# Score blocks of two directions in one TensorE run, and small products on VectorE instead of GpSimd, in a bidirectional recurrent mixer

## The chip, the cores and the metric

The kernel runs on one core of a Trainium2 chip. A core has a matrix engine (TensorE, PE in the profile, its weight loads PEld), VectorE (DVE), ScalarE (ACT), GpSimd (POOL), and queues that issue transfers between the main memory and the on-chip memories (SBUF, and PSUM for matrix products). The metric is the device time of one execution in microseconds (us).

## The reference

Two layers of a trunk: layer 0 mixes tokens by windowed attention, layer 1 by a bidirectional gated linear recurrence (HGRN2). Each mixer also carries four cross-attention heads into 256 memory tokens, and each layer ends with a convolutional feed-forward part. The change is in layer 1's mixer alone. There are 1024 tokens and 8 heads, with 128 keys and 128 values a head.

```python
def gla_chunked(q, k, v, log_f):          # chunks of 16 tokens
    b = jnp.cumsum(log_f, axis=2)
    q_dec, k_dec, k_end = q * jnp.exp(b), k * jnp.exp(-b), k * jnp.exp(b[:, :, -1:] - b)
    s = jnp.where(causal, jnp.einsum('bcthk,bcshk->bchts', q_dec, k_dec), 0.0)
    o_intra = jnp.einsum('bchts,bcshv->bcthv', s, v)
    # step over the chunks: o_inter = q_dec @ state; state = exp(b_end) * state + k_end^T v
    return o_intra + o_inter

o = gla_chunked(q, k_f, v, lf_f) + flip_t(gla_chunked(flip_t(q), flip_t(k_b), flip_t(v), flip_t(lf_b)))
o = rmsnorm(o, norm_g) * silu(gate)
```

with `f = lb + (1 - lb) * sigmoid(z)`, `log_f = log(f)`, `k = 1 - f` for each of the two directions (z from a projection of its own), and `q` passed through silu.

## The kernel before

**Stages.** The program does the memory's keys and values, layer 0's mixer (`window`), its output projection and feed-forward part, then layer 1's mixer (`hgrn`, from about 1205 to 1872 us), its output projection (`wo1.finish`) and the second feed-forward part. The large products split each fp32 operand into a high and a low part and take three products (`mm3`, lines 84 to 86). Their weights are split on arrival: ScalarE casts the high part (line 79), VectorE subtracts (line 80).

**A head of the mixer.** `proj(h)` makes queries, the two gates' inputs (`proj_fm`) and, for two heads at a time, values and output gates (`proj_tm`) into PSUM banks `pj`. ScalarE and VectorE take them out (lines 1091 to 1093, 1113, 1115, 1129, 1134). `head(h)` then goes through four directions: (forward, first half of the tokens), (backward, second half), (forward, second half), (backward, first half); `d` is 0 for forward and 1 for backward, `b` the half. After that it makes the outputs of the two halves (`output`). In every second head, cross-attention units run behind the third and the fourth direction (`cross`).

**A direction** works on 512 tokens, as four quarters `c` of 128, tokens along the free axis and the 128 keys on the partitions. ScalarE and VectorE make the decays inside chunks of 16: `EP` from the chunk's start, `ER` to its end (lines 1177 to 1192). The scores inside a quarter are built from blocks of decay levels. `E1`, `E2` (lines 1204 to 1209) hold decayed queries and keys for the 32 x 32 diagonal blocks. `step(n)` (lines 1219, 1220) doubles the length over which `ER` and `EP` reach. After it, a tile `G` holds in its later halves the decayed queries (line 1227, on GpSimd) and in its earlier halves the decayed keys (line 1228, on VectorE): `G32` for blocks between neighbours of 32 tokens, `G` for blocks between neighbours of 64.

`block(c, i, j, x, y, n)` (line 1212) is one product of 128 rows by 32 stationary columns. It writes PSUM partitions i to i+31 and n columns from j of quarter c, in the direction's bank `PA[d]`, and sits at array columns i to i+31: the array's columns are used as four groups of 32, at i = 0, 32, 64 and 96. Per quarter there are two blocks of 64 columns (from `G`), four diagonal ones of 32, and two of 32 (from `G32`). `lt` and `er` are 1 and 0 for a forward direction and 0 and 1 for a backward one. So the blocks of `G` lie in the groups at 0 and 32 for forward and at 64 and 96 for backward; those of `G32` lie at 0 and 64 for forward and at 32 and 96 for backward.

After the blocks VectorE copies the causal part of the bank to `Az[d]` (`copy_predicated`, line 1253). `As[b]`, the sum of both directions' scores, takes it: a ScalarE copy for the first direction of a half (line 1257), a GpSimd addition for the second (line 1259). GpSimd also makes the decayed query `qin` (line 1251). A transpose of the decayed key, products with the values and the state updates `S` follow (lines 1262 to 1276). `output` multiplies `As`, `qin` and `S` (line 1291) and normalizes.

**Buffers.** `E()` gives one of five tiles of the tag "E" in turn: a direction takes eight (`a_`, `L1`, `R`, `B`, `E1`, `E2`, `G32`, `G`), and one is reused when its last reader is done. `PA` is one bank for each direction, `As` has two tiles.

**What sets the order.** The code is written once, head after head. A planner with a timeline of its own (`schedule_with_timeline_sim=True`) then gives each engine a fixed order from its own estimates of durations; engines wait on semaphores. `tc.high_priority(AHEAD)` lets instructions go ahead of others that are ready, and `tc.issue_after(x)` keeps instructions behind `x` in the order.

Of the kernel before, what the change touches and what calls it, by code (L numbers as in the profile page):

```python
# [8 lines left out]
F32 = mybir.dt.float32  # L9
F32R = mybir.dt.float32r  # L10
# [3 lines left out]
ALU = mybir.AluOpType  # L14
# [4 lines left out]
P = 128  # L19
# [30 lines left out]
def build(tc, A, out):  # L50
    nc = tc.nc
    act, dve, pool, pe = nc.scalar, nc.vector, nc.gpsimd, nc.tensor
# [970 lines left out]
    def hgrn():  # L1023
# [3 lines left out]
        early = tc.alloc_tile_pool(name="hg0", bufs=1, reuse_waits="tile")  # L1027
# [4 lines left out]
        late = tc.alloc_tile_pool(name="hgv", bufs=1, side="right", reuse_waits="tile")  # L1032
        V, G = [late.tile([P, 3, NT, P], F32, name=x) for x in ("v", "gs")]
        wp = tc.alloc_tile_pool(name="hg1", bufs=1, side="right", reuse_waits="tile")
        for x in ("xh", "xl", "ph", "pl"):
            wp.tile([P, 512], F32R, tag=x, bufs=1, name=x)
        for x in ("kvh", "kvl"):
            wp.tile([P, 2, 256], F32R, tag=x, bufs=1, name=x)
# [120 lines left out]
            r["run"] = run  # L1159
            return r  # L1160

        def direction(h, r, d, b, qin, S, As):

            q, k = r["q"][b], r["s"][d][b]
            rev = slice(None, None, -1) if d else slice(None)
# [2 lines left out]
            def E():  # L1168
                return early.tile([P, 512], F32, tag="E", bufs=5, name="E")
# [51 lines left out]

            for n in (32, 64):
                step(n // 2)
                G = E()
                gl, ge = halves(G, n)
                pl_, pe_, rl_, re_, ql, qe, kl, ke = parts(n)
                pool.tensor_tensor(gl, pl_, ql, op=ALU.mult)
                dve.tensor_tensor(ge, re_, ke, op=ALU.mult)
                if n == 32:
                    G32 = G  # L1230
            with tc.high_priority(AHEAD):
                far, near, x = er * 64 + er * 32, er * 64 + lt * 32, lt * 64
                mm = None
                for c in range(4):
                    with tc.issue_after(mm.ins) if mm else nullcontext():
                        block(c, far, x, G, G, 64)
                        block(c, near, x, G, G, 64)
                        for o in (0, 32):
                            block(c, x + o, x + o, E2, E1)
                        mm = block(c, x + er * 32, x + lt * 32, G32, G32)  # L1240
                for c in range(4):
                    with tc.issue_after(mm.ins):
                        block(c, far, far, E2, E1)
                        block(c, near, near, E2, E1)
                        mm = block(c, far, near, G32, G32)
            step(64)
            dec = wp.tile([P, 4], F32, tag="dec", bufs=2, name="dec")
            e = 0 if d else P - 1
# [1 line left out]
            bs = slice(b * 512, (b + 1) * 512)  # L1250
            sum_steps[1].send(pool.tensor_tensor(qin[:, bs], EP, q, op=ALU.mult))
            dve.tensor_tensor(ER, ER, k, op=ALU.mult)
            dve.copy_predicated(Az[d], gm[d], pa.rearrange("p c t -> p (c t)"))
            a2 = lambda x: x.rearrange("p c t -> p (c t)")
            if As[b] is None:
                As[b] = wp.tile([P, 4, P], F32, tag="As", bufs=2, name="As")
                act.copy(a2(As[b]), Az[d])
            else:
                pool.tensor_tensor(a2(As[b]), a2(As[b]), Az[d], op=ALU.add)
            tp = bank("pt")  # L1260
            for c in range(4):
                pe.transpose(tp[:, c, :], ER[:, c * P:(c + 1) * P], ident)
# [5 lines left out]
            for c in (range(3, -1, -1) if d else range(4)):  # L1268
                cg = 4 * b + c
                nx = cg - 1 if d else cg + 1  # L1270
                if not 0 <= nx < NT:
                    continue
                if cg == (NT - 1 if d else 0):
                    act.copy(S[:, nx, :], pu[:, c, :])
                else:
                    dve.scalar_tensor_tensor(S[:, nx, :], S[:, cg, :], dec[:, c:c + 1], pu[:, c, :],
                                             op0=ALU.mult, op1=ALU.add)

        def output(h, r, b, qin, S, As):
            po = bank("po")  # L1280
# [45 lines left out]

        def cross(n):
            def pair(kind, i):
                return [wp.tile([P, 512], F32R, tag=kind + c, bufs=1, name=kind + c) for c in "hl"]

            for _ in range(n):
                xh_, xb_ = units.pop(0)
                if xhead[1] != xh_:
                    xhead[1] = xh_
                    xhead[0] = cross_head(1, xh_, wp)
                cross_unit(1, xh_, xb_, xhead[0], wp, tags, wp, pair, not units)

        def head(h, r):
            qin = [wo1.wf.tile([P, T], F32, tag=f"qin{d}", bufs=1, name="qin") for d in range(2)]
            S = [wp.tile([P, NT, P], F32, tag=f"S{d}", bufs=1, name="S") for d in range(2)]  # L1340
            As = [None, None]
            for i, (d, b) in enumerate(((0, 0), (1, 1), (0, 1), (1, 0))):
                direction(h, r, d, b, qin[d], S[d], As)
                if i < len(r["later"]):
                    r["run"](r["later"][i])
                cross(HX[h][i])
                if h == 7 and i == 1:
                    wo1.load(0, n=RING)
            if h == 7:
                early.release()  # L1350
                es.release()
                eq.release()
                wo1.open()
            for i, b in enumerate((1, 0)):
                output(h, r, b, qin, S, As)
                cross(HX[h][4 + i])
# [220 lines left out]
```

## Time and profile before

| | |
|---|---|
| median of 3 runs | 2629.17 us (2628.51 to 2630.56) |
| profiled execution, its own time | 2632.24 us |
| its span, first to last instruction | 2630.4 us |
| TensorE busy in the span | 2593.7 us, 99% |
| mixer of layer 1, 1205 to 1872 us: TensorE, VectorE, ScalarE, GpSimd busy | 658.31, 523.60, 354.51, 175.28 us |
| score blocks (line 1212), TensorE busy | 36.4 us, 2048 records |

A row of groups reads: line, engine, operation, output<-inputs, shapes, count | busy time in us, mean of one in ns | idle time of the engine just before, and what ended it. A row of stretches gives the length and then the busy time of each engine with its number of instructions, the granted TensorE clock (1.00 is full), the share of the transfer engines and GB/s. A row in order of time gives start, duration, engine, line, operation and count. A product in fp32 leaves two records, one for each pass.

### The profile page before, as it was taken

To read this page: it belongs to the slowest core of one execution; us is meant where nothing else is said; L and a number is where in the kernel's file an instruction comes from. 1 tells how busy PE (TensorE), PEld (TensorE's weight loads), DVE (VectorE), ACT (ScalarE), POOL (GpSimd) and SP (SyncE) were. 2 spreads that over 40 slices of the span, in tenths; PEclk is the share of its full clock that TensorE was granted. 3 is DMA by queue.
4 is the path that set the end of the run, shared out by engine and by line. 5 is a ranking of instruction groups with operands and counts; after the bars stand their busy time and mean duration, and the time that the engine had idled before them with its cause. 6 is when DMAs were issued, how large, how long until landed. Compare 5 with 4: busy or idle time off the path is not lost. (4 is left out here: it accounts for less than half of the span.)

```text
span 2630.4 us, 39132 instructions
## 1 busy us (share of the span) xinstructions
PE 2593.7 (99%) x14596; PEld 2174.2 (83%) x14596; DVE 1763.4 (67%) x2807; ACT 1333.4 (51%) x2395; POOL 476.4 (18%) x552
## 2 busy tenths in 40 slices
PE   8999999999999999999999999999999999999998
PEld 7988887888888888887888888888887888888887
DVE  6677775577555664488697796877657665656447
ACT  6566665444444454465555554556434444444453
POOL 0431110211111100032233131222311011110013
PEclk9999999999999999999999999999999999999999
DMA  9782341567787757673246341113337777775666
GB/s 356 258 199 67 103 146 57 168 171 195 192 210 201 198 160 250 194 267 109 70 151 162 75 99 47 55 49 101 120 119 197 190 201 200 205 200 172 215 193 236
DMA packets 203919, 431.18 MB, mean 164 GB/s; under 512 B 20048, under 2 KB 64464, under 8 KB 198096
## 3 DMA queue, kind: packets, MB, share of 16 engines
q1 hardware_dynamic: 169744, 329.30, 38.4%
q0 software_dynamic: 24544, 90.19, 16.4%
q10 hardware_dynamic: 9440, 9.19, 1.1%
q8 instruction: 114, 1.87, 0.3%
q14 instruction: 77, 0.63, 0.1%
HBM read 333.18 MB, written 119.54 MB: 172 GB/s over the span
## 5 line engine op out<-in xcount | busy, mean ns | idle before, releaser
L90 DVE TENSOR_TENSOR wl<-st,wh 128x1024 fp32r<-128x1024 f32 (+1 forms) x238 | 263.3, 1113 | 318.8 <-ACT wh L89 294.4
L89 ACT CAST wh<-st 128x1024 fp32r<-128x1024 f32 (+1 forms) x238 | 222.6, 937 | 293.1 <-PE X L578 194.1
L84 PE MATMUL pj<-uh,wh 128*128 128x512 f32 x512 | 202.9, 397 | 3.6 <-DVE q L1129 2.5
L578 PE MATMUL X<-wl,wh 128*128 128x512 f32 x528 | 204.7, 390 | 0.3 <-DVE wl L90 0.3
L578 PE MATMUL X<-wh,wl 128*128 128x512 f32 x528 | 204.5, 389 | 0.0
L86 PE MATMUL pj<-uh,wl 128*128 128x512 f32 x512 | 202.1, 395 | 0.0
L85 PE MATMUL pj<-ul,wh 128*128 128x512 f32 x512 | 201.0, 393 | 0.1
L578 PE MATMUL X<-wh 128*128 128x512 f32 x528 | 198.7, 390 | 1.4 <-ACT c L992 1.4
L84 PE MATMUL pj<-wh,uh 128*128 128x384 f32 (+1 forms) x512 | 189.0, 370 | 2.5 <-DVE gs L1115 1.9
L86 PE MATMUL pj<-wh,ul 128*128 128x384 f32 (+1 forms) x512 | 187.1, 365 | 0.0
L85 PE MATMUL pj<-wl,uh 128*128 128x384 f32 (+1 forms) x512 | 187.0, 365 | 0.0
L80 DVE TENSOR_TENSOR wl<-st,wh 128x1024 fp32r<-128x1024 f32 (+1 forms) x91 | 119.1, 1316 | 29.7 <-ACT wh L79 28.9
L578 PE MATMUL V<-uh,wh 128*128 128x512 f32 x336 | 130.7, 389 | 0.0
L578 PE MATMUL V<-ul,wh 128*128 128x512 f32 x336 | 130.7, 389 | 0.0
L578 PE MATMUL V<-uh,wl 128*128 128x512 f32 x336 | 130.7, 389 | 0.0
L578 PEld LDWEIGHTS X<-wh 128*128 128x128 f32 x528 | 99.1, 188 | 22.4 <-ACT c L992 1.8
L578 PEld LDWEIGHTS X<-wl,wh 128*128 128x128 f32 x528 | 99.1, 188 | 21.1 <-DVE wl L90 0.7
L578 PEld LDWEIGHTS X<-wh,wl 128*128 128x128 f32 x528 | 99.1, 188 | 20.5
L84 PEld LDWEIGHTS pj<-uh,wh 128*128 128x128 f32 x512 | 96.3, 188 | 23.4 <-DVE q L1129 3.3
L79 ACT CAST wh<-st 128x1024 fp32r<-128x1024 f32 (+1 forms) x97 | 97.5, 1014 | 35.3 <-PE pj L85 22.3
L961 POOL TENSOR_TENSOR c<-c,g 128x512 f32<-128x512 f32 x24 | 42.5, 1789 | 391.2 <-PE X L578 322.1
L85 PEld LDWEIGHTS pj<-ul,wh 128*128 128x128 f32 x512 | 96.3, 188 | 19.3 <-DVE ul L90 0.4
(409 smaller groups left out, 7058.8 us busy)
## 6 DMA issues: line engine op xcount, KB each, us to landing
st<-hid SPq DMA_DIRECT2D x154, 256.0 KB, 3.0
st<-in_ffw_dram SPq DMA_DIRECT2D x108, 256.0 KB, 3.2
w2s<-in_ffw_dram POOLq DMA_DIRECT2D x24, 1024.0 KB, 8.3
st<-in_ffw_dram SPq DMA_DIRECT2D x46, 512.0 KB, 4.2
hid<-tt SPq DMA_DIRECT2D x88, 256.0 KB, 4.8
st<-w2s SPq DMA_DIRECT2D x88, 256.0 KB, 2.8
sx<-in_ffw_dram SPq DMA_DIRECT2D x84, 256.0 KB, 3.9
sy<-in_ffw_dram SPq DMA_DIRECT2D x42, 512.0 KB, 6.6
```

The source lines that it names most:

```text
L79: act.copy(h[:, :n], raw)
L80: (eng or dve).tensor_tensor(l[:, :n], raw, h[:, :n].bitcast(F32), op=ALU.subtract)
L84: pe.matmul(o, ah, bh, start=first, stop=False)
L85: pe.matmul(o, ah, bl, start=False, stop=False)
L86: return pe.matmul(o, al, bh, start=False, stop=last)
L89: act.copy(h, src)
L90: dve.tensor_tensor(l, src, h.bitcast(F32), op=ALU.subtract)
L578: last = pe.matmul(o, x, y, start=new, stop=e, skip_group_check=not first)
L961: pool.tensor_tensor(y[q][:, t, :], y[q][:, t, :], g3[:, c], op=ALU.mult)
```

## The change

Directions are now taken in pairs: (forward, first half) with (backward, second half), and (forward, second half) with (backward, first half).

- The first of a pair issues only its 16 diagonal blocks. It returns three functions: `tops` (its blocks of `G`), `mids` (its blocks of `G32`) and `masked` (the masked copy and the sum). `head` hands them to the second as `held`.
- The second issues one run: its own first `tops`, then quarter by quarter the held `tops`, its own `tops`, its own four diagonal blocks, the held `mids` and its own `mids`. Both maskings follow, the held one first. The number of blocks stays 32 a direction.
- The first of a pair keeps its `G32` and `G` in a new tag "H" with two tiles, so that it takes six tiles of "E"; the second takes eight as before. The room comes from cross-attention's `ph` and `pl`, which now share the tiles of `xh` and `xl`.
- The product of decay and query into `G` goes from GpSimd to VectorE and stands behind the one of the keys (64 instructions of 128 x 256). The addition into `As` goes from GpSimd to VectorE (16 of 128 x 512). `qin` stays on GpSimd.

```diff
-        for x in ("xh", "xl", "ph", "pl"):
+        for x in ("xh", "xl"):
             wp.tile([P, 512], F32R, tag=x, bufs=1, name=x)
...
-        def direction(h, r, d, b, qin, S, As):
+        def direction(h, r, d, b, qin, S, As, held):
...
             for n in (32, 64):
                 step(n // 2)
-                G = E()
+                G = E() if held else early.tile([P, 512], F32, tag="H", bufs=2, name="H")
                 gl, ge = halves(G, n)
                 pl_, pe_, rl_, re_, ql, qe, kl, ke = parts(n)
-                pool.tensor_tensor(gl, pl_, ql, op=ALU.mult)
                 dve.tensor_tensor(ge, re_, ke, op=ALU.mult)
+                dve.tensor_tensor(gl, pl_, ql, op=ALU.mult)
                 if n == 32:
                     G32 = G
+            def tops(c):
+                return [block(c, er * 64 + t * 32, lt * 64, G, G, 64) for t in (er, lt)][-1]
+
+            def mids(c):
+                return [block(c, o + er * 32, o + lt * 32, G32, G32) for o in (0, 64)][-1]
+
             with tc.high_priority(AHEAD):
-                far, near, x = er * 64 + er * 32, er * 64 + lt * 32, lt * 64
-                mm = None
+                if held:
+                    mm = tops(0)
                 for c in range(4):
-                    with tc.issue_after(mm.ins) if mm else nullcontext():
-                        block(c, far, x, G, G, 64)
-                        block(c, near, x, G, G, 64)
-                        for o in (0, 32):
-                            block(c, x + o, x + o, E2, E1)
-                        mm = block(c, x + er * 32, x + lt * 32, G32, G32)
-                for c in range(4):
-                    with tc.issue_after(mm.ins):
-                        block(c, far, far, E2, E1)
-                        block(c, near, near, E2, E1)
-                        mm = block(c, far, near, G32, G32)
+                    with tc.issue_after(mm.ins) if held or c else nullcontext():
+                        if held:
+                            held[0](c)
+                            if c:
+                                tops(c)
+                        for o in range(0, P, 32):
+                            mm = block(c, o, o, E2, E1)
+                        if held:
+                            held[1](c)
+                            mm = mids(c)
             step(64)
...
+            def masked():
+
+                dve.copy_predicated(Az[d], gm[d], pa.rearrange("p c t -> p (c t)"))
+                a2 = lambda x: x.rearrange("p c t -> p (c t)")
+                if As[b] is None:
+                    As[b] = wp.tile([P, 4, P], F32, tag="As", bufs=2, name="As")
+                    act.copy(a2(As[b]), Az[d])
+                else:
+                    dve.tensor_tensor(a2(As[b]), a2(As[b]), Az[d], op=ALU.add)
+
+            if held:
+                held[2]()
+                masked()
             tp = bank("pt")
...
+            return None if held else (tops, mids, masked)
...
             def pair(kind, i):
-                return [wp.tile([P, 512], F32R, tag=kind + c, bufs=1, name=kind + c) for c in "hl"]
+                return [wp.tile([P, 512], F32R, tag="x" + c, bufs=1, name=kind + c) for c in "hl"]
...
+            held = None
             for i, (d, b) in enumerate(((0, 0), (1, 1), (0, 1), (1, 0))):
-                direction(h, r, d, b, qin[d], S[d], As)
+                held = direction(h, r, d, b, qin[d], S[d], As, held)
```

The lines taken out between `dve.tensor_tensor(ER, ER, k, ...)` and `tp = bank("pt")` are the former masking and sum, now in `masked`, with the addition on `pool`.

More of the change, by code (lines that the diff above doesn't have):

```diff
@@ L1252, in direction @@
             dve.tensor_tensor(ER, ER, k, op=ALU.mult)
[L1253 to L1259, printed above, removed]
+            def masked():
[9 more added lines that the diff above has]
+                masked()
             tp = bank("pt")
```

## The prediction

> **What bounds the kernel now.** I read the page first, then the busy time by stage, then the groups of the touched lines, then one run of the score blocks in order of time.
>
> ```profile
> span 2630.4 us, 39132 instructions
> PE 2593.7 (99%) x14596; PEld 2174.2 (83%) x14596; DVE 1763.4 (67%) x2807; ACT 1333.4 (51%) x2395; POOL 476.4 (18%) x552
> ...
> core 0: us, PE busy (x) PEld busy (x) DVE busy (x) ACT busy (x) POOL busy (x), PEclk, DMA share, GB/s
> 1205.00:1872.00 667.00, 658.31 (x5226) 555.82 (x5225) 523.60 (x981) 354.51 (x759) 175.28 (x183) 1.00 0.30 87
> ```
>
> TensorE is busy for 99% of the span. The recurrent mixer, the only stage that the change touches, lies between 1205 and 1872 us. There TensorE works 658.31 of 667.00 us at full clock and idles 8.69 us. A microsecond taken off TensorE in this stage is therefore a microsecond off the end, so long as no other engine takes over. VectorE stands second at 523.60/667 = 78.5%, but unevenly:
>
> ```profile
> 1306.00:1402.00 96.00, 95.47 (x866) 81.81 (x866) 88.63 (x170) 56.66 (x128) 33.98 (x39) 1.00 0.38 132
> 1474.00:1570.00 96.00, 91.69 (x845) 78.07 (x844) 84.90 (x162) 52.81 (x124) 33.53 (x36) 1.00 0.45 107
> 1642.00:1738.00 96.00, 94.45 (x854) 80.22 (x853) 87.12 (x169) 54.33 (x127) 27.96 (x30) 1.00 0.16 53
> ```
>
> Each of these three stretches holds six of the 32 directions (the 32 runs of blocks start between 1230 and 1866 us), and VectorE is 88 to 92% busy in them. This is where VectorE could take over.
>
> **The score blocks on TensorE.** A direction forms its scores in 32 small products (line 1212), each recorded as two passes: 64 records in one unbroken run, each on 32 columns of the array.
>
> ```profile
> 1399.16 0.27 PE L1302 MATMUL pt<-ident,on 128*128 128x128 f32 x1
> 1399.37 1.14 PE L1212 MATMUL pa<-E 128*32 128x64 f32 x64
> 1401.03 0.47 PE L84 MATMUL pj<-wh,uh 128*128 128x512 f32 x1 [0.53 <-DVE gs L1115]
> ...
> L1212 PE MATMUL pa<-E 128*32 128x32 f32 (+1 forms) x2048 | 36.4, 205 | 1.9 <-POOL E L1227 1.9
> ...
> L1212 PE MATMUL pa<-E 128*32 128x32 f32 x1536 | 36.0, 199 | 0.0
> L1212 PE MATMUL pa<-E 128*32 128x64 f32 x512 | 20.5, 222 | 1.9 <-POOL E L1227 1.9
> ```
>
> The run takes 1.14 us and all 32 take 36.4, so 1.14 is what every run costs. One record takes 0.20 us, 64 in sequence would be 13 us; the four groups of 32 columns work side by side. Count the moving columns that each group gets. In the first loop, per quarter c, `far` and `near` get a block of 64 each, the other two get 32, and one of these another 32 (G32). In the second loop `far` gets 32+32, `near` 32, the other two nothing. The group of `far` so streams 4 x (64+32+32) = 512 columns; the rest less. If that longest group sets the run, 1.14 - 0.20 (the last record) = 0.94 us for 512 columns, 1.84 ns a column.
>
> After the change the same blocks are dealt out otherwise. First direction of a pair: four diagonal blocks of 32 per quarter, one to each group, 128 columns a group: 128 x 1.84 + 0.20 = 0.43 us. Second direction: per quarter the 64-wide blocks of both directions fill all four groups (a forward one has its `far` and `near` in the lower two, a backward one in the upper two), then the four diagonal blocks, then four G32 blocks: 64+32+32 = 128, over four quarters 512: 1.14 us as before. A pair costs 1.57 instead of 2.28 us; 16 pairs save 16 x 0.71 = **11.3 us**.
>
> The bound on the other side is the rate at which records can start, since the second run packs 96 of them.
>
> ```profile
> core 0: us, PE busy (x) PEld busy (x), PEclk, DMA share, GB/s
> 1399.30:1399.42 0.12, 0.06 (x4) 0.06 (x8) 1.00 0.00 0
> 1399.30:1399.84 0.54, 0.47 (x39) 0.48 (x42) 1.00 0.00 0
> ```
>
> In the first 0.47 us 39 products start, 12 ns each; at that rate 96 need 1.16 + 0.20 = 1.36 us and a pair saves 0.49, 7.8 us in all. But 8 weight loads start within the first 0.06 us (7 ns each), so starting is hardly the limit; I take 11.3.
>
> The Trainium skill ("TensorE: Matmul & The Clock Gate", section "Part 3: Packing small matmuls — row/col tiling") says that products start strictly in program order, though on different tiles they overlap. By that rule the second pass of a block would hold back every later block, the run would go by the number of blocks, and this regrouping would save nothing. The trace does not look like it: four products start within the first 0.06 us, although the second record in program order is the second pass of the first block, which has to wait for 64 x 1.84 / 2 = 59 ns of columns.
>
> **Products and addition moved to VectorE.**
>
> ```profile
> L1227 POOL TENSOR_TENSOR E<-EP,q 128x256 f32<-128x256 f32 x64 | 54.7, 855 | 287.2 <-DVE EP L1220 262.1 <-ACT gs L1091 11.7 <-ACT E L1177 6.9
> L1251 POOL TENSOR_TENSOR qin<-EP,q 128x512 f32<-128x512 f32 x32 | 47.0, 1467 | 49.9 <-PE po L1291 39.2 <-DVE EP L1220 10.7
> L1259 POOL TENSOR_TENSOR As<-As,Az 128x512 f32<-128x512 f32 x16 | 26.0, 1628 | 25.6 <-DVE Az L1253 25.5
> ...
> L1219 DVE TENSOR_TENSOR ER<-ER,EP 128x256 f32<-128x256 f32 x96 | 60.7, 633 | 1.2
> L1182 DVE TENSOR_TENSOR E<-E 128x512 f32<-128x512 f32 x32 | 37.4, 1168 | 2.1 <-ACT E L1179 1.8
> L1228 DVE TENSOR_TENSOR E<-ER,s 128x256 f32<-128x256 f32 x64 | 26.7, 417 | 0.0
> L1187 DVE TENSOR_TENSOR E<-E 128x512 f32<-128x512 f32 x32 | 22.0, 688 | 0.8
> L1252 DVE TENSOR_TENSOR ER<-ER,s 128x512 f32<-128x512 f32 x32 | 21.8, 681 | 0.0
> ```
>
> GpSimd loses 54.7 + 26.0 us. VectorE gains 64 products at 0.417 us (line 1228, same shape) and 16 additions at 0.681 (line 1252): 26.7 + 10.9 = 37.6 us. But it also gets something back. Line 1219 has line 1228's shape and takes 633 instead of 417 ns; line 1182 has line 1187's and takes 1168 instead of 688. Why shows in order of time:
>
> ```profile
> 1261.69 1.79 DVE L1182 TENSOR_TENSOR E<-E 128x512 f32<-128x512 f32 x1
> ...
> 1261.29 1.64 POOL L1259 TENSOR_TENSOR As<-As,Az 128x512 f32<-128x512 f32 x1 [1.44 <-DVE Az L1253]
> ...
> 1426.35 0.83 DVE L1219 TENSOR_TENSOR ER<-ER,EP 128x256 f32<-128x256 f32 x1
> ...
> 1426.12 0.77 POOL L1227 TENSOR_TENSOR E<-EP,q 128x256 f32<-128x256 f32 x1 [0.95 <-DVE EP L1220]
> ```
>
> A two-input VectorE instruction that starts inside a GpSimd one lasts until 0.3 to 0.5 us past its end. The excess of the two lines is 96 x 0.216 + 32 x 0.480 = 36 us. Laying every long VectorE instruction beside GpSimd's, I find 48 of line 1219 inside line 1227 (0.365 us lost each, 17.5 us) and 11 of line 1182 inside line 1259 (1.1 us each, 12.1 us), with 2 us on the weight splits: about 31.7 us caused by the instructions that move, the rest by `qin` (line 1251), which stays. The net load on VectorE is 37.6 - 31.7 = **+5.9 us**, 0.18 per direction, 529.5 us in the stage.
>
> The Trainium skill ("SBUF — State Buffer", section "Who interferes with whom") names this: a VectorE instruction with two SBUF inputs and a GpSimd instruction that reads SBUF take one port pair in turn, the later one blocked to the end of the first. The trace agrees (1.79 us against 0.69).
>
> The 5.9 us lie beside TensorE outside the dense stretches. Inside them fall 18 directions, 3.3 us of load. I charge TensorE **+2.5 us**, between 0 (all covered) and what the slower rival gives.
>
> TensorE waited 1.9 us at line 1212 for GpSimd's product. Now the product follows line 1228's on VectorE: 0.42 + 0.42 us after the decay's own step, against 0.86 on GpSimd. I take **-1.0** (0 to -1.9).
>
> **What is moved or renamed, at nothing.** The held direction's masking and sum (line 1253, 0.73 us, and what follows) come one direction later, directly ahead of the second one's. Queued behind them on VectorE are the state updates and the next direction's start; waiting for them is the first product of `output`. TensorE has the next head's projections to do meanwhile; without that cover each of 8 heads would wait for 0.73 + 0.68 us, 11 us. The H tiles let the next direction's first buffers come free earlier (ScalarE's line 1178 waits 11.9 us for blocks today), which costs nothing. Cross attention's `ph`, `pl` sharing `xh`, `xl` makes a unit's query split wait for the unit before; units lie a direction apart (some 13 us), so nothing. No DMA is added or moved; those that follow `qin` on GpSimd's queue find it freer.
>
> **The sum.** The profiled execution took 2632.24 us, 1.84 above its span; the median of the runs is 2629.17, 3.07 lower. 2632.24 - 11.3 - 1.0 + 2.5 = 2622.4 for such an execution, 2619.4 for the median: **2619.5 us**.
>
> **The rivals.**
>
> *VectorE caps the dense stretches (2625.5 us).* At +0.18 a direction the first would carry 88.63 + 1.1 = 89.7 us of VectorE work in 96.0 - 2.1 = 93.9 us, 95.5%. The highest share of any stretch that long is 92.3%. With that as cap it takes 97.2 (+1.2), the third 95.6 (-0.4), the second still gains 2.1, the 14 other directions 4.9: -6.2, and 2.5 for new waits. For: TensorE's wait for line 1115 in the dense part (0.53 above). Against: 12 us windows there reach 99%.
>
> *Starts in program order (2630.7 us).* If a block waits for all blocks ahead of it, a run goes by its number of blocks, 64 a pair before and after: no saving, and only the two small terms stay, +1.5. The four starts in 0.06 us speak against it.
>
> *Slower: the collisions move to `qin` (2637 us).* It stays on GpSimd, 32 times, and 80 more two-input instructions on VectorE can meet it. If all that was credited comes back there, the load is +37.6. Each dense stretch gets 12 products and 3 additions, 7.05 us: 95.7, 92.0 and 94.2 us. With a cap of 95% that is +4.7, +0.8 and +3.1, less 4.9 elsewhere: +3.7, still no loss that shows. With 92.3% it is +7.7, +3.6, +6.1 less 4.9: +12.5. It decides from about 94.5%; the middle is +8. For: `qin` at 1467 ns mean collides already. Against: where it now begins, line 1252 runs at 681 ns untouched.
>
> *More than forecast (2613 us).* The two directions are less tied to each other and half of the 8.7 us of idle TensorE goes too: -11.3 - 4.4.
>
> **How the numbers follow.** Forecast 0.50 (its own range 2614 to 2624), capped 0.17, program order 0.06, slower 0.14, more 0.13. What this kernel's measurement can tell from no change is about 0.2%, 5.3 us: faster is below 2623.9, slower above 2634.4. Forecast and "more" give 0.63, less a little for a new order of instructions by the planner: faster 0.62, same 0.24, slower 0.14. The range runs from the middle of "more" to half way into "slower": 2611 to 2635.
>
> **What would show it.** Line 1212's busy time falls from 36.4 to about 25 us, in 16 short runs of 32 records (0.43 us) and 16 of 96 (1.14). Line 1219 falls to about 0.45 us mean, line 1182 to about 0.8, VectorE's stage sum rises to some 530. If the 96-record runs take 1.4 us or more, the column count was the wrong measure. If TensorE's idle time in the stage grows beyond 12 us with VectorE named as releaser, the dense stretches were the bound. If `qin` sits over long VectorE instructions in most directions, the slower rival holds.

## The result, and the profile after

| | before | after |
|---|---|---|
| median of 15 runs | 2628.51 us (2626.16 to 2630.56) | 2634.55 us (2630.39 to 2637.82) |
| ratio of times | | 1.0022, 95% interval 1.0015 to 1.0029 |
| profiled execution, its own time | 2632.24 us | 2630.39 us |
| granted TensorE clock, mean over the runs | 0.9987 (26 runs of the experiments' first session) | 0.9970 (15 runs) |

The changed kernel is 6.0 us **slower**; 2619.5 us was forecast. The profiled execution is the fastest of the 15, and the only one with a mean clock of 0.999, so a part of the loss is not in the trace below. Executions that ran far slower than the others of their kernel, such as the profiled one of e11 (4344 us), are left out of the medians and rows below. The page of the kernel after:

```profile
span 2628.6 us, 39039 instructions
PE 2587.2 (98%) x14596; PEld 2162.1 (82%) x14596; DVE 1753.3 (67%) x2887; ACT 1332.6 (51%) x2395; POOL 396.5 (15%) x472
```

Its busy time by stretch, with the stage and the three dense stretches in the places the prediction used (engine busy times, then the clock):

```profile
core 0: us, PE busy (x) PEld busy (x) DVE busy (x) ACT busy (x) POOL busy (x), PEclk, DMA share, GB/s
1205.00:1872.00 667.00, 653.40 (x5222) 545.00 (x5221) 516.17 (x1061) 354.14 (x757) 95.53 (x103) 1.00 0.30 88
1306.00:1402.00 96.00, 93.52 (x852) 78.58 (x851) 85.62 (x181) 58.24 (x129) 21.31 (x26) 1.00 0.35 125
1474.00:1570.00 96.00, 93.53 (x831) 78.20 (x830) 83.12 (x176) 53.12 (x113) 21.16 (x22) 0.98 0.42 100
1642.00:1738.00 96.00, 93.48 (x839) 77.99 (x838) 83.29 (x181) 55.61 (x117) 17.89 (x16) 1.00 0.15 50
```

TensorE idles 667.00 - 653.40 = 13.6 us of the stage, 8.7 before. VectorE is busy for **less** time: 516.17 against 523.60 us, and 85.6, 83.1, 83.3 against 88.6, 84.9, 87.1 in the dense stretches. So an engine was given more instructions, its busy time fell, and TensorE waits more. The groups of instructions show that the parts worked as intended:

```profile
L1219 DVE TENSOR_TENSOR ER<-ER,EP 128x256 f32<-128x256 f32 x96 | 40.3, 420 | 0.1
L1212 PE MATMUL pa<-E 128*32 128x32 f32 (+1 forms) x1536 | 26.1, 201 | 0.0
...
L1182 DVE TENSOR_TENSOR E<-E 128x512 f32<-128x512 f32 x32 | 21.9, 684 | 0.9 <-ACT E L1179 0.9
...
L1212 PE MATMUL pa<-H 128*32 128x64 f32 (+1 forms) x512 | 18.6, 210 | 0.0
```

Line 1219 fell from 633 to 420 ns and line 1182 from 1168 to 684: on these two lines the collisions with GpSimd are gone, 20.4 + 15.5 us, against 64 products and 16 additions of some 37 us. Those with `qin` stayed and fell on other lines: 12 VectorE instructions of the mixer take 0.2 us or more over their usual time beside it, 11.2 us in all, where there were 16 and 13.7 us. One of them, of 0.42 us when undisturbed:

```profile
1362.00 1.41 DVE L1207 TENSOR_TENSOR E<-ER,s 128x256 f32<-128x256 f32 x1
...
1361.84 1.29 POOL L1256 TENSOR_TENSOR qin<-EP,q 128x512 f32<-128x512 f32 x1
```

The durations of all VectorE instructions of the stage add up to 586.1 us, 580.9 before: 5.3 more. The busy time falls all the same, because it counts once the time in which two records overlap: instructions of 0.42 us that follow each other start every 0.34 us (lines 1220 and 1227 in the first gap below).

Nothing waits at line 1212 any more (1.9 us before). Its two rows overlap in time, so the blocks are read from the runs, in order of time:

```profile
1224.43 0.46 PE L1212 MATMUL pa<-E 128*32 128x32 f32 x32
...
1237.53 0.25 PE L1212 MATMUL pa<-E 128*32 128x64 f32 x2
1237.54 0.25 PE L1212 MATMUL pa<-H 128*32 128x64 f32 x2
1237.61 0.23 PE L1212 MATMUL pa<-E 128*32 128x64 f32 x2
1237.62 0.23 PE L1212 MATMUL pa<-H 128*32 128x64 f32 x2
...
1238.50 0.20 PE L1212 MATMUL pa<-H 128*32 128x32 f32 x1
```

A first direction's run takes 0.46 us, a second one's 1238.70 - 1237.53 = 1.17 us. All 32 alternate like this: 16 x (0.46 + 1.17) = 26.1 us where there were 36.4. The 10.3 us are really saved, and they do not arrive at the end. Where they go is told by TensorE's waits in the stage, 1205 to 1872 us (line waited for: us in total, times, longest). Before:

```profile
PE pj L84 <- DVE q L1129: 2.5, 2, 2.3
PE pj L84 <- DVE gs L1115: 1.9, 3, 0.7
PE pa L1212 <- POOL E L1227: 1.9, 4, 0.7
PE pj L84 <- DVE s L1134: 1.0, 1, 1.0
```

After:

```profile
PE pj L84 <- DVE s L1134: 8.4, 4, 2.5
PE pt L1273 <- ACT ot L1333: 1.3, 1, 1.3
PE po L84 <- ACT ph L89: 1.2, 4, 0.3
PE po L85 <- DVE pl L90: 0.9, 4, 0.2
PE pj L84 <- DVE gs L1115: 0.6, 1, 0.6
```

The first line is new: three gaps of 2.5 us, one in each dense stretch, at 1360.6, 1522.5 and 1688.7 us. The projections have two `pj` banks. A bank comes free when line 1134 has taken its content out, and in these gaps line 1134 stands late in VectorE's queue. The first gap in order of time:

```profile
1354.76 0.42 DVE L1219 TENSOR_TENSOR ER<-ER,EP 128x256 f32<-128x256 f32 x1
1355.09 0.69 DVE L1180 SCALAR_TENSOR_TENSOR s<-s,E 128x512 f32<-128x512 f32 x1
1355.69 0.69 DVE L1182 TENSOR_TENSOR E<-E 128x512 f32<-128x512 f32 x1
1356.30 0.42 DVE L1220 TENSOR_TENSOR EP<-EP 128x256 f32<-128x256 f32 x1
1356.63 0.42 DVE L1227 TENSOR_TENSOR H<-ER,s 128x256 f32<-128x256 f32 x1
1356.97 1.22 DVE L1184 TENSOR_TENSOR_SCAN E<-smask,E 128x512 f32<-128x512 bf16 x1
...
1359.01 0.69 DVE L1187 TENSOR_TENSOR E<-E 128x512 f32<-128x512 f32 x1
...
1359.87 0.69 DVE L1134 TENSOR_SCALAR s<-pj 128x512 f32<-128x512 f32 x1
...
1361.14 0.69 DVE L1257 TENSOR_TENSOR ER<-ER,s 128x512 f32<-128x512 f32 x1
...
1357.74 0.40 PE L86 MATMUL pj<-uh,wl 128*128 128x512 f32 x1
1360.62 0.50 PE L84 MATMUL pj<-uh,wh 128*128 128x512 f32 x1 [2.48 <-DVE s L1134]
```

VectorE is busy without a hole. But lines 1180, 1182, 1184 and 1187 belong to the pair's **second** direction; they are its opening, 0.69 + 0.69 + 1.22 + 0.69 = 3.3 us, and they stand between the last steps of the **first** (1219, 1220, 1227, 1228, and 1257, which makes its decayed key). So the first direction's decayed key (line 1257) comes only at 1361.14, TensorE has no transposes of it to do in the meantime, and nothing is left but the projection whose bank is not free.

Before, the opening came behind the decayed key (line 1252 there):

```profile
1354.54 0.68 DVE L1252 TENSOR_TENSOR ER<-ER,s 128x512 f32<-128x512 f32 x1
...
1359.67 0.68 DVE L1180 SCALAR_TENSOR_TENSOR s<-s,E 128x512 f32<-128x512 f32 x1
```

That is so in all 16 pairs of the kernel before: the second direction's scan (line 1184) starts 4.8 to 9.8 us behind the first one's decayed key. In the kernel after it starts ahead of it in 11 of 16. By the code, the opening needs tiles of the tag "E" that the first direction's blocks had to read first. With `G32` and `G` in tiles of their own, and with the diagonal blocks of the first direction issued at once, those tiles come free early, and the planner uses it. No run has the regrouping without the tiles H, so this last link is argued from the code.

### The profile page after: what moved, and what is told of

The parts are those of the page before. It is cut to its first block, busy times and chain, and to the rows that moved or that the text cites. A ratio compares the mean times of both kernels' runs of the same rounds, so it can differ in the third digit from the quotient of the medians.

```text
span 2628.6 us, 39039 instructions
## 1 busy us (share of the span) xinstructions
PE 2587.2 (98%) x14596; PEld 2162.1 (82%) x14596; DVE 1753.3 (67%) x2887; ACT 1332.6 (51%) x2395; POOL 396.5 (15%) x472
## 5 line engine op out<-in xcount | busy, mean ns | idle before, releaser
L90 DVE TENSOR_TENSOR wl<-st,wh 128x1024 fp32r<-128x1024 f32 (+1 forms) x238 | 261.5, 1105 | 319.3 <-ACT wh L89 301.4
L80 DVE TENSOR_TENSOR wl<-st,wh 128x1024 fp32r<-128x1024 f32 (+1 forms) x91 | 111.7, 1233 | 30.2 <-ACT wh L79 28.9
L84 PEld LDWEIGHTS pj<-uh,wh 128*128 128x128 f32 x512 | 96.6, 189 | 31.3 <-DVE s L1134 10.1
L86 PEld LDWEIGHTS pj<-uh,wl 128*128 128x128 f32 x512 | 96.6, 189 | 19.5 <-issue 0.4
```

The lines of the kernel that those rows point to most:

```text
L80: (eng or dve).tensor_tensor(l[:, :n], raw, h[:, :n].bitcast(F32), op=ALU.subtract)
L84: pe.matmul(o, ah, bh, start=first, stop=False)
L86: return pe.matmul(o, al, bh, start=False, stop=last)
L90: dve.tensor_tensor(l, src, h.bitcast(F32), op=ALU.subtract)
```

## The experiments

Two theories stood at the start. *Load*: VectorE carries too much, so taking work off it helps. *Order*: the work is not too much, but the second direction's opening overtakes the first one's end. All kernels compute the whole reference; ratios are to the kernel before in the same session. Its median lay between 2628.4 and 2629.0 us in the sessions, so a difference between kernels of two sessions is good to about 0.7 us. "Mixer and output projection" below is the time from the mixer's first projection product to the first product of the feed-forward part.

| kernel | median, us (runs) | ratio, 95% interval |
|---|---|---|
| e1_regroup: after, products and addition on GpSimd | 2661.47 (4) | 1.0124, 1.0110 to 1.0137 |
| e2_moves: before, products and addition on VectorE | 2635.53 (11) | 1.0025, 1.0015 to 1.0034 |
| e3_held_back: after, first opening step held back | 2636.73 (11) | 1.0024, 1.0015 to 1.0033 |
| e4_share: before, shared tiles in cross attention | 2628.35 (11) | 0.9998, 0.9989 to 1.0007 |
| e5_opening: after, whole opening held back | **2624.86** (11) | 0.9986, 0.9977 to 0.9994 |
| e6_tail: after, first direction's end preferred | 2636.98 (7) | 1.0025, 1.0014 to 1.0036 |
| e7_regroup_opening: e5, products and addition on GpSimd | 2644.05 (5) | 1.0058, 1.0044 to 1.0072 |
| e8_first_on_pool: e5, first direction's products on GpSimd | 2641.25 (5) | 1.0046, 1.0033 to 1.0058 |
| e9_qin_first: e5, `qin` ahead of `dec` | **2624.42** (11) | 0.9984, 0.9975 to 0.9993 |
| e10_moves_opening: e2 with the opening held back | 2634.92 (11) | 1.0022, 1.0013 to 1.0031 |
| e11_add_on_pool: e5, addition on GpSimd | 2629.71 (10) | 1.0003, 0.9994 to 1.0012 |
| e12_products: before, products alone on VectorE | 2638.14 (5) | 1.0036, 1.0023 to 1.0050 |

**The parts one by one: e1, e2, e4.** The kernel after with the old engines:

```diff
+                pool.tensor_tensor(gl, pl_, ql, op=ALU.mult)
                 dve.tensor_tensor(ge, re_, ke, op=ALU.mult)
-                dve.tensor_tensor(gl, pl_, ql, op=ALU.mult)
...
-                    dve.tensor_tensor(a2(As[b]), a2(As[b]), Az[d], op=ALU.add)
+                    pool.tensor_tensor(a2(As[b]), a2(As[b]), Az[d], op=ALU.add)
```

> The regrouping alone: blocks of both directions in one run, the H tiles and the shared cross-attention tiles, but the product of decay and query and the scores' addition stay on GpSimd. Order theory (the second direction's opening goes ahead of the first one's last step on VectorE, so qin, the query tile and the projection's bank come free late): line 1212 falls to some 24 us as in the changed kernel, and the TensorE gaps of about 2.5 us at the projections of heads 1, 3 and 5 stay, three of them; time 2628 to 2637 us, ratio 1.000 to 1.003. Load theory (the 80 instructions moved to VectorE make it late): the gaps go, time 2617 to 2622 us, ratio 0.996 to 0.998.

It is 32 us slower than before, far beyond what either theory gave. TensorE's waits of e1, from 1195 to 1990 us:

```profile
PE pj L84 <- DVE gs L1115: 12.1, 3, 6.0
PE pt L1273 <- DVE ER L1257: 7.5, 3, 2.6
```

VectorE is the releaser again, though 80 instructions were taken from it. They did not make it lighter: over the mixer and output projection it is busy for 596.8 us, 592.8 after, since GpSimd's products collide with its instructions again. So e1 cannot tell the two theories apart. Nearly half of the 32 us is clock: in its profile TensorE runs at half clock for nine times 3.4 us in that stretch, 15.4 us lost. The reverse, the moves without the regrouping:

```diff
-                pool.tensor_tensor(gl, pl_, ql, op=ALU.mult)
                 dve.tensor_tensor(ge, re_, ke, op=ALU.mult)
+                dve.tensor_tensor(gl, pl_, ql, op=ALU.mult)
...
-                pool.tensor_tensor(a2(As[b]), a2(As[b]), Az[d], op=ALU.add)
+                dve.tensor_tensor(a2(As[b]), a2(As[b]), Az[d], op=ALU.add)
```

> The moves alone: the kernel before with the product of decay and query and the scores' addition on VectorE; blocks, buffers and sums ordered as before. Order theory: no new gaps; the 4 us of TensorE waits for GpSimd's product go in part, VectorE's collisions go; time 2624 to 2629 us, ratio 0.998 to 1.000. Load theory: VectorE comes late, gaps of 2 us or more at the projections of heads 1, 3 and 5; 2631 to 2637 us, ratio 1.001 to 1.003.

The moves alone cost 6.5 us. That is the time which the load theory gave, but not its gaps: those of 2.5 us do not appear, and VectorE is busy for 596.5 us over the mixer and output projection, 601.8 before. In place of the gaps stand smaller waits at the ends of heads (e2, same view):

```profile
PE pj L84 <- DVE gs L1115: 3.2, 3, 1.1
PE pb L84 <- ACT oh L89: 2.7, 2, 1.9
```

So there are two losses: one that comes with the regrouping and one that comes with the moves. The shared tiles alone:

```diff
-        for x in ("xh", "xl", "ph", "pl"):
+        for x in ("xh", "xl"):
...
-                return [wp.tile([P, 512], F32R, tag=kind + c, bufs=1, name=kind + c) for c in "hl"]
+                return [wp.tile([P, 512], F32R, tag="x" + c, bufs=1, name=kind + c) for c in "hl"]
```

> The kernel before with one edit: cross-attention's probabilities share the two tiles of its queries. If the sharing costs nothing, as the prediction has it: 2627 to 2630 us, ratio 0.999 to 1.001. If it causes the changed kernel's new TensorE waits of 0.29 and 0.23 us ahead of the value products in each even head: these appear here, 4 x 0.95 us, 2631 to 2634 us, ratio 1.001 to 1.002.

It makes the two small waits of the kernel after at lines 84 and 85 (1.2 and 0.9 us in e4, as after), and yet costs nothing that can be measured.

**The order: e3, e5, e6, e9.** First one instruction of the opening (line 1180) was held behind the first direction's last step:

```diff
-            dve.scalar_tensor_tensor(k, k, -1.0, L1, op0=ALU.mult, op1=ALU.subtract)
+            with tc.issue_after(held[3].ins) if held else nullcontext():
+                dve.scalar_tensor_tensor(k, k, -1.0, L1, op0=ALU.mult, op1=ALU.subtract)
...
-            step(64)
+            grown = step(64)
```

(`step` returns its last instruction, and the first of a pair returns `grown` as `held[3]`.)

> The changed kernel, but VectorE's opening of a pair's second direction (line 1180) is kept in the order behind the first one's last step. Order theory: the third and the fourth qin of a head lie 12 us or more apart again instead of 7 to 9, the three gaps of 2.5 us go, the mean granted clock of the runs rises from 0.997 to 0.998 or more; time 2618 to 2625 us, ratio 0.996 to 0.999. Load theory: the gaps stay or move, since the work is the same; 2630 to 2637 us.

The three gaps stay (2.54, 2.55, 2.44 us). The scan of line 1184 does not depend on line 1180, so it still went ahead, in 11 of 16 pairs as after: the edit did not do what it was for, and decides nothing. In e5 the other entry (line 1182, which the scan reads) is held as well:

```diff
+            with tc.issue_after(held[3].ins) if held else nullcontext():
                 dve.scalar_tensor_tensor(k, k, -1.0, L1, op0=ALU.mult, op1=ALU.subtract)
                 act.activation(k, k, AF.Exp, bias=lno[:, d, h:h + 1])
                 dve.tensor_tensor(a_, a_, L1, op=ALU.subtract)
```

> The changed kernel with all of VectorE's opening of a pair's second direction (its first two instructions, on which the scan and the rest hang) kept behind the first direction's last step; the earlier try held only one of the two and the scan still went ahead. Order theory: the third and fourth qin of a head come 12 us or more apart, the three gaps of 2.5 us at the projections go, granted clock 0.998 or more, time 2618 to 2625 us, ratio 0.996 to 0.9985. Rival (the gaps come from somewhere else, for instance from the held direction's own longer chain, or from VectorE's added work): three gaps of 2 us or more stay, 2630 to 2638 us.

2624.86 us: 9.7 less than after, and 4.1 less than the kernel before in the same session. No scan of a second direction starts ahead of the first one's decayed key any more. The same place in e5 in order of time (its lines from 1181 on are one higher):

```profile
1357.81 0.69 DVE L1258 TENSOR_TENSOR ER<-ER,s 128x512 f32<-128x512 f32 x1
1358.41 0.69 DVE L1181 SCALAR_TENSOR_TENSOR s<-s,E 128x512 f32<-128x512 f32 x1
1359.01 0.69 DVE L1183 TENSOR_TENSOR E<-E 128x512 f32<-128x512 f32 x1
...
1359.87 0.69 DVE L1134 TENSOR_SCALAR s<-pj 128x512 f32<-128x512 f32 x1
...
1358.64 0.63 PE L1274 MATMUL pt<-ident,ER 128*128 128x128 f32 x4
1360.61 0.50 PE L84 MATMUL pj<-uh,wh 128*128 128x512 f32 x1 [1.34 <-DVE s L1134]
```

The decayed key now comes at 1357.81 instead of 1361.14. Line 1134 starts at 1359.87 as in the kernel after; it is TensorE that now has the four transposes ahead of the wait, so that 1.34 of 2.48 us remain. That is so in all three places (1.34, 1.34, 1.35 us); the gaps shrink, they do not go.

This decides between the theories: over the mixer and output projection VectorE is busy for 592.9 us in e5 and 592.8 after. The load is the same, the order is not. In the profiled executions that stretch takes 787.9 us in e5 and 794.3 after. Of these 6.4 us, 3.4 are the shorter gaps and 1.7 the clock. Of the 9.7 us between the medians some 4 are clock, 0.9986 on the mean in e5 against 0.9970.

In e6 the first direction's end was preferred to other ready work, instead of holding the opening back:

```diff
-            step(64)
+            with nullcontext() if held else tc.high_priority(AHEAD):
+                step(64)
```

(with `dec`, `qin` and the product of line 1257 inside it).

> The changed kernel with a high priority on the first direction's last step, its qin and its decayed key (they go ahead of other work that is ready). Order theory: the same remedy from the other end, but the second direction's opening can still go ahead of the steps before; gaps shorter than 2.5 us, 2624 to 2631 us. Rival: as the changed kernel, 2632 to 2637 us.

The order hardly changed (the scan is ahead in 11 of 16 pairs as after), and the gaps stayed (2.48, 2.49, 2.46 us). What e6 shows is the **clock**. Its profiled execution is 2637.81 us, 7.4 above that of the kernel after, with nearly the same waits. Around its first gap, by stretch:

```profile
1358.20:1360.70 2.50, 0.02 (x2) 0.01 (x1) 2.50 (x8) 1.52 (x4) 0.00 (x0) 1.00 0.00 0
1360.85:1364.25 3.40, 3.40 (x9) 2.65 (x10) 3.40 (x8) 1.20 (x3) 2.81 (x4) 0.51 0.00 0
1364.40:1367.40 3.00, 3.00 (x14) 2.39 (x13) 2.90 (x9) 1.23 (x3) 0.00 (x0) 1.00 1.01 341
```

After an idle 2.5 us TensorE runs at half clock for 3.4 us: 9 products, where 14 fit in the next 3.0 us. That costs 1.7 us. The record of the clock has five such stretches in this execution between 1205 and 1990 us, one in that of the kernel after (at 1523.8, right behind its second gap) and none in the mixer before: four more are 6.8 of the 7.4 us.

In e9, `qin` goes ahead of `dec` on GpSimd, so that the query tile comes free earlier:

```diff
-            pool.tensor_copy(dec.unsqueeze(2), ...)
-            sum_steps[1].send(pool.tensor_tensor(qin[:, bs], EP, q, op=ALU.mult))
+            done = pool.tensor_tensor(qin[:, bs], EP, q, op=ALU.mult)
+            with tc.issue_after(done.ins):
+                pool.tensor_copy(dec.unsqueeze(2), ...)
+            sum_steps[1].send(done)
```

> As e5_opening, and on GpSimd qin goes ahead of the small decay copy (line 1254 of the changed kernel) instead of behind it, so that the query tile comes free 0.6 to 1.7 us earlier. If the late query tile is the link by which the projection's bank is held, the three gaps shrink from 1.34 us to below 0.7: 2621 to 2624 us, about 2 us below e5_opening. If the bank waits for VectorE's queue alone, the gaps stay at 1.3 us: 2623 to 2627 us.

2624.42 us, with 1.34 us gaps as in e5: what remains of the wait is VectorE's queue, not the query tile. It is the fastest of all, though not to be told from e5.

**Load, once more: e7, e8, e11.** All three are e5 with instructions moved from VectorE back to GpSimd. e7 carries e1's diff, e11 only its last two lines, and e8 this:

```diff
+                if not held:
+                    pool.tensor_tensor(gl, pl_, ql, op=ALU.mult)
                 dve.tensor_tensor(ge, re_, ke, op=ALU.mult)
-                dve.tensor_tensor(gl, pl_, ql, op=ALU.mult)
+                if held:
+                    dve.tensor_tensor(gl, pl_, ql, op=ALU.mult)
```

> The regrouping alone (products of decay and query and the scores' addition on GpSimd) with the second direction's opening held back as in e5_opening. Order theory: most of the 32 us that the regrouping alone lost comes back, since the opening went far ahead of a chain made long by GpSimd's products: 2622 to 2634 us. Rival (GpSimd's products and their collisions themselves cost the 32 us): it stays above 2650 us.

> As e5_opening, but the first direction of a pair makes its products of decay and query on GpSimd, the second on VectorE. Order theory: VectorE is not the bound, and a chain through GpSimd is longer by 0.4 us a step; within 4 us of e5_opening, rather slower. Load theory: VectorE loses 13 us of work, so 2 us or more faster than e5_opening.

> As e5_opening, but the scores' addition stays on GpSimd (the products of decay and query on VectorE). Theory that a GpSimd instruction costs VectorE more than it relieves it: 11 of line 1182's instructions are long again by 1.1 us, nothing else; 1 to 5 us slower than e5_opening, 2626 to 2630 us. Load theory: VectorE loses 10.5 us of work, 1 to 4 us faster, 2621 to 2624 us.

They are 19.2, 16.4 and 4.9 us **slower** than e5. e7 against e1 shows the worth of the order once more: holding the opening back gives 17.4 us there. But that is only half of what e1 lost, and the 2622 to 2634 us that the order theory gave were missed by 10. It missed e8 by more than 10 as well.

Nor do these runs test the load theory, for VectorE did not get lighter by them. Over the mixer and output projection it is busy for 604.3 us in e7 and 599.9 in e8, against 592.9 in e5, although 80 and 32 instructions fewer run on it. e8 shows why at its three gaps, which are 2.42 us long again. In each, line 1183, two places ahead of line 1134 in VectorE's queue, takes 1.75 us instead of the 0.69 in e5, because `qin` runs beside it (1359.97 to 1361.69 us, line 1183 from 1360.48, in the first gap). These 1.06 us are nearly all of the 1.08 by which the gap is longer. The rest of the 16 us is spread: 5.1 are clock. The expectation of e11, that a GpSimd instruction costs VectorE more than it relieves it of, gave its time rightly.

**The moves: e10, e12.** e10 is e2 with the opening held back as in e5:

> The moves alone with the second direction's opening held back as in e5_opening, blocks as before. It differs from e5_opening by the regrouping with its tiles alone. If the regrouping is worth what line 1212 shows (10.3 us less), this takes 8 to 12 us more than e5_opening: 2633 to 2637 us. If e5_opening gained by the order of the opening alone: 2623 to 2628 us.

2634.92 us, as e2. So holding back does nothing without the regrouping, where the opening came behind anyway, and e5 less e10, **-10.1 us**, is what the regrouping with its tiles is worth. That agrees with the 10.3 us of line 1212. e12 is e2 without the addition's move:

> The kernel before with only the products moved (the decay-query product stands on VectorE behind the decay-key product; the addition into As stays on GpSimd). Both moves together cost 6.5 us on the kernel before. If the products carry that, because 64 instructions of 0.42 us now stand in VectorE's queue ahead of the evacuations of the projections' banks (lines 1113, 1115, 1134), this one stays 5 to 7 us slower than before, 2634 to 2636 us. If the addition carries it, because it puts VectorE work at the end of each half ahead of the head's evacuations, this one is within 1.5 us of before, 2627.5 to 2630.5 us. By the prediction's own pricing (collisions go away as the load comes) it would also be the latter.

The products alone cost 9.8 us, more than both moves together. In the profiled execution of e12 the largest wait between 1195 and 1990 us is one at the end of the mixer (same view of waits):

```profile
PE pb L84 <- ACT oh L89: 5.8, 1, 5.8
```

There the last head's outputs come late to the output projection; in the ten microseconds before, VectorE does four weight splits (line 80) among the last direction's state updates. Half clock for 6.8 us begins inside this wait. Why the order comes out worse with the products on VectorE was not isolated further. In e2, e10 and e12 some 2 to 3 us of the loss are clock: means of 0.9975, 0.9976 and 0.9976, against 0.9987, 0.9984 and 0.9987 for the kernel before in the same sessions.

## Why the prediction was wrong

| step of the prediction | forecast | the runs |
|---|---|---|
| regrouped blocks, by columns a group | -11.3 us | -10.3 (line 1212), -10.1 (e5 less e10) |
| wait for GpSimd's product at line 1212 | -1.0 | -1.9 (the wait is gone) |
| VectorE's load in the stage | +5.9 | +5.3 by durations added up; busy time -7.4 (523.60 to 516.17) |
| charged to TensorE for it | +2.5 | +6.2 to +9.8 (e10, e2, e12) |
| shared tiles of cross attention | 0 | -0.7 (e4; nothing measurable) |
| tiles free earlier for the next direction | 0 | **+9.7** (after less e5) |

Put end to end: before to e10 +6.2, e10 to e5 -10.1, e5 to after +9.7, together +5.8 us, where 6.0 were measured. (It must close: each step starts where the last one ends, and 0.2 us lie between sessions.) The split holds for this path only: the same moves cost 6.5 us without the regrouping, and are worth 19.2 with it and the opening held back (e7 to e5).

**Right: the blocks.** The runs of 32 and 96 records take 0.46 and 1.17 us where 0.43 and 1.14 were worked out. The column groups run side by side, and not in program order: in the rows of the long run two passes from `H` start at 1237.54, ahead of two from `E` at 1237.61, although by the code the direction's own first blocks, four passes from `E`, stand ahead of those from `H`. At the record rate a long run would have taken 1.36 us.

**The step that failed:** "The H tiles let the next direction's first buffers come free earlier [...], which costs nothing." A buffer that is late was read as a loss only. Here it was also what kept the second direction behind the first in VectorE's queue. Freed, its opening overtook the first one's end by 3.3 us in the place shown, and the price lies on TensorE, in gaps and in clock. e5 undoes the overtaking with VectorE's busy time unchanged and gets 9.7 us back. The prediction allowed "a little" for a new order of instructions in its chances, and nothing in its sum. Forecast and result lie 15.7 us apart: 9.7 are this step, 4.7 the moves (6.2 where 2.5 - 1.0 were forecast) and 1.2 the blocks.

**Wrong in size: the moves.** The load itself was worked out well: +5.3 us by durations, +5.9 forecast. It was then added to the busy time (529.5 us), which counts overlaps once and came out at 516.2. What failed is the step from there to TensorE: 2.5 us were charged, and 6.2 to 9.8 were paid by kernels in which VectorE is busy for less time than before (596.5 us in e2 and e10, 599.6 in e12, 601.8 before, over the mixer and output projection). So the price is not in the load. A part of it is clock; the rest probably lies in where the planner put the evacuations of banks, which no run isolates.

**The signs that were named.** Line 1212, the two runs, lines 1219 and 1182 came out as forecast or better; VectorE's busy time of some 530 us did not. TensorE's idle time passed the 12 us with VectorE as releaser (13.6, 8.4 of it at line 1134). That was to mean that VectorE bounds the dense stretches; the sign appeared and its reading was false, for VectorE's busy time in them fell, and e5 waits less with the same busy time. The "slower" rival needed the credited collisions to come back at `qin`; 12 of 32 `qin` lie beside a long instruction, 16 before. The measured time lies inside the range and near that rival, but for another reason: that is luck. Program order, by which a pair would still take 2.28 us, is excluded by 0.46 + 1.17 = 1.63. The rival "the two directions are less tied" had the right fact and the wrong sign.

**The clock.** The mean clock of 0.9970 against 0.9987 is 0.0017 x 2630 = 4.5 us of lost clock a run. The runs of the kernel after go from 2630.4 us at 0.999 to 2636.0 at 0.996 (means of 1 and 6 runs). From the mixer's first projection product to the first product of the feed-forward part the profiled executions take 792.7 us before and 794.3 after, 1.7 of the latter lost at half clock. So in the trace the saved blocks are just eaten by waits and later starts, and most of the 6 us in the median are stretches at half clock that this execution happened to be spared.

**Open:** the named waits of the stage grew by only some 5 us, and about as much again of the lost 10 is spread over products that start a little later each, without a releaser; it was not traced further. Also open are the remaining 1.34 us of each gap in e5, and what the moves cost without the regrouping beyond the 2 to 3 us of clock.

## What to carry to other kernels

A buffer that an engine waits for may be what keeps a later stage of work behind an earlier one in an in-order queue: before freeing it, ask what will then go ahead, and of what, and hold that back in the order (here one `issue_after` was worth 9.7 us). When the busy sum of an engine falls and others wait for it more, look at the order of its instructions and not at its load. With TensorE at 99%, price a new gap at its length plus the slow clock that can follow it (here 1.7 us), and compare many runs, since one profile can miss it.

## What the hardware showed that was not expected

**Short gaps cost clock.** In the profiles of the kernel after, e1, e3, e6 and e8 there are 15 gaps of 2.4 to 2.6 us on TensorE between 1350 and 1720 us; with nine of them 3.4 us at half clock begin, between 0.3 us before the gap's end and 2.1 us behind it, with six not, and the same code does either: 1 of 3 in the kernel after, none in e3, all three in e6. After the six gaps of 1.34 us in e5 and e9 there is none. The length of the gap alone does not decide, since e6 has one behind a 1.26 us gap. The Trainium skill ("TensorE: Matmul & The Clock Gate", section "Part 1: The HAM clock gate (the "warmup" mystery)") says that the clock is set by the activity in windows of 3413 ns that run freely. The 3.4 us stretches agree, and so does where they stand: within an execution they begin whole multiples of 3.413 us apart (in e6 48, 16, 33 and 55 of them).

A gap's position in these windows explains why it varies. Cut on that grid, 1195 to 2040 us of the 13 profiles other than e11's hold 3170 windows at full clock. In 24 of them TensorE idled for 1.85 us or more, and the next window was at half clock each time. In 3124 it idled for less than 1.46 us, and the next never was. Of the 22 between, eight were followed by half clock. So a gap of 2.5 us costs 1.7 us more if enough of it falls into one window, and nothing more if it is split between two; one of 1.34 us is too short alone, and the 1.26 us of e6 shared their window with other idle time, 1.82 us in all.

The Trainium skill ("TensorE: Matmul & The Clock Gate", section "Why this matters for your kernels") advises against idle gaps of more than about 3 us. That is too mild here: 2.5 us cost 1.7 us more in nine cases of 15.

**A collision can cost more than the work.** Moving 37 us of two-input work from GpSimd to VectorE made VectorE's busy time 7.4 us smaller, with fewer collisions between the two. Moving 32 products, 13 us, back to GpSimd (e8 against e5) made it 7.0 us larger.
